# Layer 0's row maxima over 1024 keys at a time, ahead of each tile's scores, with value sums, totals and turns in the score banks

## The chip, the cores and the metric

One core of one Trainium2 chip runs the whole kernel. The metric is the device time of one execution in microseconds (us). The kernel is written in Bass and Tile: Tile places the tiles, records which instruction must wait for which, and sets semaphores; in layer 0's attention the order on TensorE (PE), VectorE (DVE) and ScalarE (ACT) is the order of the code, while GpSimd (POOL) and the DMA queue of SyncE (SP) are ordered by Tile's scheduler.

## The reference

Two attention layers over 1024 latent tokens and 256 context tokens of width 1024. Layer 0 is grouped-query attention with 16 heads of 64 and 4 key heads; a context token sees context keys only.

```python
def gqa_attend(q, k, v):
    s = jnp.einsum('bqhgd,bkhd->bhgqk', q, k).astype(jnp.float32) * (GQA_HEAD_DIM ** -0.5)
    p = jax.nn.softmax(s, axis=-1).astype(v.dtype)
    return jnp.einsum('bhgqk,bkhd->bqhgd', p, v)
...
    k_all = jnp.concatenate([kc, k], axis=1)
    v_all = jnp.concatenate([vc, v], axis=1)
    o = sweep_query_blocks(lambda qb: gqa_attend(qb, k_all, v_all), q).reshape(B, S, GQA_WIDTH)
    y = (o * jax.nn.silu(g)) @ p["w_out"]
...
        oc = gqa_attend(qc, kc, vc).reshape(B, L, GQA_WIDTH)
```

Around it stand RMS norms, projections, a SiLU gate and the output projection. Layer 1 is latent attention with 16 heads. Inputs and outputs are 32-bit floats.

## The kernel before

The attention of a layer is a list of units. Layer 0 has 20: 16 latent units, one for each head (10 key tiles of 128 keys against 1024 queries), and 4 context units, one for each key head (2 key tiles, 256 queries of 4 heads). They run as four latent units, one context unit, four, one, eight, and two context units at the end.

**A key tile.** `scores_by_halves` forms the scores, transposed: 128 keys by 1024 queries in a tile `st` of two PSUM banks, from a pool of two such tiles (`ps_s`). Each operand is split into a high and a low part of 64 rows, and the two halves of the queries lie on the two row halves of PE. So a tile has four products for each half (`QH,KA`, `QH,KB`, `QL,KA`, and `shift,minus`, which subtracts the row maximum), and a product of one half runs beside one of the other. ACT then writes the exponentials `p` out of `st` (line 508), which frees that buffer.

**The maxima.** The row maximum of a query over its keys is needed before the unit starts. The steps for units to come are cut into pieces and set between the products of the current unit (`next_maxima`, `max_parts`): one step is a product of 128 queries with 512 keys into a one-bank tile `mx` (`ps_m`, three of them), and a reduce over 512 on DVE. A latent unit has 16 such steps and 4 for the context keys, a context unit 4. Each key tile takes two steps, one for each row half: the one ahead of the first product of its half, the other behind the second product of the other half.

**The turn.** When a unit's maxima are done, `do_shift` reduces them to one value for each query; at the end of the unit that runs then, `turn` transposes them with PE into an `mx` tile (line 422), DVE casts them into the row `crow` (line 424, one buffer), and two small DMAs write the row into the unit's `shift` tile (line 427). There are four such tiles, used in turn.

**The end of a unit.** In this order: the turns; `pair_sum` on DVE, which adds the last four `p` by twos (line 528, four reduces); the totals of the unit before (line 597: PE sums the added `p` over the partitions into an `mx` tile, DVE transposes the result, line 601, and takes the reciprocal `cr`, line 602); then the value sums of this unit (`do_av`, line 555: 40 rows of the profile into the one-bank tile `av` of `ps_o`, one buffer), and `finish`, where ACT copies `av` to `os`. POOL adds the first six `p` and the pair sums meanwhile (`acp`, line 542), and scales the results.

Layer 0's PSUM is 3 banks of `ps_m`, 4 of `ps_s` and 1 of `ps_o`. While the gates before the attention are computed, `at.maxima` takes 36 steps ahead, and the unit loop starts with `at.run(28, 3, ...)`.

Of the kernel before, what the change touches and what calls it, by code (L numbers as in the profile page):

```python
# [26 lines left out]
TT = NT // P  # L27
EPS = 1e-6
HALVES = (True, True)


def raw(ap):
# [4 lines left out]
def hybrid_kernel(ctx: ExitStack, tc: tile.TileContext, ins: dict, out: bass.AP):  # L37
# [271 lines left out]
    class Attention:  # L309
        def __init__(self, l, units, ops):  # L310
            self.l, self.units, self.ops = l, units, ops
            self.state = {}
            self.vcache = {}
            self.kcache = {}
            self.sm = sm_pool
            self.step = 0
            self.deferred = []
            self.totals = []
            self.turns = []
            self.started = 0  # L320
            self.done = 0
            self.todo = []
            self.last_lat = [u for u in units if u["kind"] == "lat"][-1]
# [53 lines left out]
        def max_parts(self, u, step):  # L377
# [30 lines left out]
                return half, [part_ctx] + [lambda: None] * (self.ops["mparts"] - 1)  # L408
            return half, [lambda j=j: part(j) for j in range(self.ops["mparts"])]

        def do_shift(self, u):

            s = self.state[id(u)]
            if u["kind"] == "lat":
                m = self.sm.tile([P, 8], F32, name="m1", tag="m1")
                dve.reduce_max(m, s["m"], axis=AX.X)
            else:
                m = s["m"][:, :, 0]

            def turn():  # L420
                t = self.ps_m.tile([P, 512], F32, name="mx", tag="mx")[:8, :P]
                pe.transpose(t, m, ident)
                r = self.sm.tile([8, P], F32R, name="crow", tag="crow", bufs=1)
                dve.tensor_copy(r, t)
                if HALVES[self.l]:
                    for n in range(2):
                        sp.dma_start(raw(s["crow"][n]), raw(r[4 * n:4 * n + 4, :]))
                else:
                    sp.dma_start(raw(s["crow"]), raw(r))

            self.turns.append(turn)

        def start_unit(self):
            u = self.units[self.started]
            s = self.ops["load"](u, self)
            lat = u["kind"] == "lat"
            s["m"] = self.sm.tile([P, 8, 3 if lat else 1], F32, name="m", tag="m" if lat else "mc")
# [3 lines left out]
            if HALVES[self.l]:  # L441
                if lat:
                    self.todo += [(u, ("lat", i + 4 * a, n)) for i in range(4) for n in range(2) for a in range(2)]
                self.todo += [(u, ("ctx", i + 2 * a, 0)) for i in range(2) for a in range(2)]
            else:
                if lat:
                    self.todo += [(u, ("lat", i, n)) for i in range(8) for n in range(2)]
                self.todo += [(u, ("ctx", i, 0)) for i in range(4)]
            self.started += 1

        def next_maxima(self, upto, limit):

            steps = []
            while self.done < upto:
                if not self.todo and self.started < min(limit, len(self.units)):
                    self.start_unit()
                if not self.todo:
                    break
                u, m = self.todo.pop(0)
                self.done += 1  # L460
                half, parts = self.max_parts(u, m)
# [30 lines left out]
        def scores_by_halves(self, u, kt, p, steps):  # L492
# [15 lines left out]
            act.activation(p, ps, AF.Exp, scale=self.ops["scale"])  # L508
# [37 lines left out]
        def do_av(self, u, group, ps):  # L546
# [1 line left out]
            s = self.state[id(u)]  # L548
            kts = u["kts"]
            if group[0] == kts[0]:  # L550
                s["av"] = self.ps_o.tile([P, 512], F32, name="av", tag="av")
                s["v"] = self.load_v(u)
            for kt, p in zip(group, ps):
                for n in range(2):
# [16 lines left out]
        def finish(self, u):  # L571
# [19 lines left out]
            cr = sm.tile([P, 8], F32, name="cr", tag="cr")  # L591

            def total():
                t = s["av"] if u is not self.units[-1] and not HALVES[l] else self.ps_m.tile([P, 512], F32, name="mx", tag="mx")
                for i, part in enumerate(s["total"]):
                    for q in range(4):
                        pe.matmul(t[32 * q:32 * q + 32, :256], lhsT=twos, rhs=part[:, q * 256:q * 256 + 256],  # L597
# [31 lines left out]
        def run(self, lead, ahead, extra, tail):  # L629
# [3 lines left out]
            with tc.manual_schedule(engines={mybir.EngineType.PE, mybir.EngineType.DVE, mybir.EngineType.Activation}):  # L633
                for t, u in enumerate(self.units):
# [13 lines left out]
                    for group in (kts[:cut], kts[cut:]):  # L648
# [560 lines left out]

    def l0_open(at, st):  # L1210
        pool_ = st.enter_context(tc.tile_pool(name="shift0", bufs=1, **right))
        at.minus = pool_.tile([P, P], F32R, name="minus")
        at.shift = [pool_.tile([P, 512], F32R, name=f"shift{i}") for i in range(4)]
        for t in (at.minus, *at.shift):
            pool.memset(raw(t), 0.0)
        for n in range(2):
            pool.memset(raw(at.minus[64 * n:64 * n + 1, :]), -1.0)

    def l0_load_halves(u, at, lat, KH, KL):
        g = u["g"]  # L1220
        i = at.started % 4
        qp = at.qp if i < 3 else at.qp2
        QH = qp.tile([P, 512], F32R, name="QH", tag="QA")
        QL = qp.tile([P, 512], F32R, name="QL", tag="QB")
        for t, src in ((QH, q0h), (QL, q0l)):
            for n in range(2):
                dst = raw(t[64 * n:64 * n + 64, :])
                if lat:
                    h = u["h"]
                    sp.dma_start(dst, src[h // 2, 64 * (h % 2):64 * (h % 2) + 64, 512 * n:512 * n + 512])  # L1230
                else:
                    sp.dma_start(dst.rearrange("p (a n) -> p a n", a=2),
                                 src[2 * g:2 * g + 2, 64 * n:64 * n + 64, NL:].rearrange("a p n -> p a n"))
        X = at.shift[i]
        return dict(KH=KH, KL=KL, QH=QH, QL=QL, X=X, minus=at.minus, crow=[X[64 * n:64 * n + 1, :] for n in range(2)])

    def l0_load(u, at):
        kp = at.kp
# [38 lines left out]

    def l0_maxima(s, n):
        r = slice(64 * n, 64 * n + 64)
        return [(s["QH"][r, :], s["KH"][r, :])]  # L1280

    def l0_scores(s, kt, n=None):
        ks = slice(kt * P, (kt + 1) * P)
        if n is not None:
            r = slice(64 * n, 64 * n + 64)
            return [(s["KH"][r, ks], s["QH"][r, :]), (s["KL"][r, ks], s["QH"][r, :]),
                    (s["KH"][r, ks], s["QL"][r, :]), (s["minus"][r, :], s["X"][r, :])]
        return [(s["KA"][:, ks], lambda n: s["QA"][:, n * 512:(n + 1) * 512]),
                (s["KB"][:, ks], lambda n: s["QB"][:, n * 512:(n + 1) * 512])]
# [511 lines left out]
```

## Time and profile before

| | |
|---|---|
| three timed runs | 1706.63, 1708.12, 1713.32 us (median 1708.12) |
| the profiled execution, its own time | 1703.22 us |
| its span | 1701.4 us |
| mean granted TensorE clock | 0.997 |
| layer 0's attention | about 380 to 750 us of the span |

A row of the timeline has the start, the time from the first start to the last end of the equal instructions that follow each other, the engine, the line, the operation, output and inputs, partitions and elements, their count, and in brackets the idle time of the engine ahead of it and what ended that. Matmuls overlap in their pipeline, so two rows that start 0.23 us apart can each show 0.39. A row of a table by windows has the stretch, its length, the busy time of PE, PE's weight loads, DVE, ACT and POOL with the number of instructions, then the granted clock, the DMA engines' share and GB/s. A row of the waits has who waited for whom, the sum, the number of times and the longest.

### The profile page before, as it was taken

What the parts mean: (1) busy time and instruction counts of PE and PEld (TensorE: products, weight loads), DVE (VectorE), ACT (ScalarE), POOL (GpSimd) and SP (SyncE); (2) the same over time, 40 slices, a digit from 0 to 9 for tenths busy, and PEclk for the clock granted to TensorE, in tenths of its full rate; (3) what the DMA queues carried; (4) which work ended last, traced back from release to release, by engine and by line L of the source; (5) the groups of instructions that cost most, each with busy time, mean ns of one, the idle gap of its engine ahead of it and who ended that gap; (6) DMA issues with size and microseconds to landing.
All of it is one profiled execution on the core that took longest, in us unless ns stands there. A gap on an engine that the chain in (4) does not pass through costs nothing. (4 is left out here: it accounts for less than half of the span.)

```text
span 1701.4 us, 27386 instructions
## 1 busy us (share of the span) xinstructions
PE 1663.7 (98%) x10212; PEld 1195.3 (70%) x10212; DVE 1042.7 (61%) x1807; ACT 641.6 (38%) x943; POOL 961.3 (57%) x646
## 2 busy tenths in 40 slices
PE   8999999999999999999989999999999999999998
PEld 5776768775555555557878889886766667667587
DVE  3765552357788777725575657754778777777231
ACT  4642222124455544432244543330434434344310
POOL 2773441218789988753235555350668787787521
PEclk9999999999999999999999999999999999999999
DMA  9557854521242422146433766776565555653451
GB/s 312 171 149 241 257 171 149 152 81 45 63 120 63 112 63 61 36 132 214 135 98 111 230 198 183 215 206 150 130 144 134 132 122 118 145 126 90 121 166 73
DMA packets 219821, 238.97 MB, mean 140 GB/s; under 512 B 23016, under 2 KB 159192, under 8 KB 219688
## 3 DMA queue, kind: packets, MB, share of 16 engines
q1 hardware_dynamic: 219264, 237.11, 49.5%
q8 instruction: 81, 1.33, 0.3%
q14 instruction: 52, 0.43, 0.1%
q10 hardware_dynamic: 424, 0.11, 0.0%
HBM read 163.37 MB, written 73.63 MB: 139 GB/s over the span
## 5 line engine op out<-in xcount | busy, mean ns | idle before, releaser
L395 DVE TENSOR_REDUCE m<-mx 128x1 f32<-128x512 f32 x512 | 336.0, 687 | 176.6 <-PE mx L393 171.6
L508 ACT ACTIVATE p<-st 128x1024 f32<-128x1024 f32 x328 | 335.9, 1027 | 170.9 <-PE st L501 137.5
L542 POOL TENSOR_TENSOR acp<-acp,p 128x1024 f32<-128x1024 f32 x128 | 305.4, 2386 | 7.8
L555 PE MATMUL av<-p,v 128*64 128x512 f32 x1312 | 289.9, 595 | 0.0
L555 PEld LDWEIGHTS av<-p,v 128*64 128x64 f32 x1312 | 90.9, 137 | 180.5 <-issue 177.9
L542 POOL TENSOR_TENSOR acp<-p 128x1024 f32<-128x1024 f32 x34 | 81.4, 2397 | 149.0 <-ACT p L508 148.9
L542 POOL TENSOR_TENSOR acp<-acp,acd 128x1024 f32<-128x1024 f32 x60 | 141.9, 2365 | 22.3 <-DVE acd L528 19.2
L528 DVE TENSOR_REDUCE acd<-p 128x512 f32<-128x1024 f32 x124 | 144.6, 1219 | 7.8 <-ACT p L508 7.8
L136 POOL TENSOR_TENSOR wb<-wraw,wa 128x512 fp32r<-128x512 f32 (+3 forms) x73 | 96.1, 1335 | 78.7 <-ACT wa L157 78.6
L93 PE MATMUL mm<-wa,hh 128*128 128x512 f32 (+2 forms) x336 | 127.2, 379 | 1.7 <-ACT hh L890 1.7
L501 PE MATMUL st<-QH,KH 64*128 64x512 f32 x320 | 122.9, 407 | 1.0 <-DVE gth L303 1.0
L95 PE MATMUL mm<-wa,hl 128*128 128x512 f32 (+2 forms) x336 | 121.3, 361 | 1.4 <-DVE hl L893 1.4
L94 PE MATMUL mm<-wb,hh 128*128 128x512 f32 (+2 forms) x336 | 120.9, 360 | 0.0
L501 PE MATMUL st<-QH,KL 64*128 64x512 f32 x320 | 119.6, 395 | 0.0
L501 PE MATMUL st<-QL,KH 64*128 64x512 f32 x320 | 118.9, 392 | 0.0
L576 ACT COPY os<-av 128x512 f32<-128x512 f32 x36 | 21.1, 587 | 255.9 <-PE av L555 214.5
L93 PE MATMUL y<-wa,oh 128*128 128x512 f32 (+1 forms) x296 | 114.3, 386 | 1.0 <-DVE yt L750 1.0
L95 PE MATMUL y<-wa,ol 128*128 128x512 f32 (+1 forms) x296 | 113.7, 384 | 0.0
L94 PE MATMUL y<-wb,oh 128*128 128x512 f32 (+1 forms) x296 | 113.7, 384 | 0.0
L404 DVE TENSOR_REDUCE m<-mx 128x2 f32<-128x512 f32 x144 | 95.4, 688 | 24.1 <-PE mx L403 19.0
L393 PE MATMUL mx<-KH,QH 64*128 64x512 f32 x256 | 102.6, 407 | 0.3 <-DVE m L404 0.3
L93 PE MATMUL mm<-hh,wa 128*128 128x512 f32 x256 | 102.1, 399 | 0.4 <-DVE qt L1675 0.4
(240 smaller groups left out, 4016.0 us busy)
## 6 DMA issues: line engine op xcount, KB each, us to landing
mraw<-in_l_w_mod SPq DMA_DIRECT2D x64, 256.0 KB
wraw<-in_l_w_in SPq DMA_DIRECT2D x28, 512.0 KB
KH<-k1h SPq DMA_DIRECT2D x32, 320.0 KB
KL<-k1l SPq DMA_DIRECT2D x32, 320.0 KB
rb<-rrow SPq DMA_DIRECT2D x72, 128.0 KB
mraw<-in_l_w_mod SPq DMA_DIRECT2D x16, 512.0 KB
sgd<-gth SPq DMA_DIRECT2D x32, 256.0 KB
wraw<-in_l_w_out SPq DMA_DIRECT2D x16, 512.0 KB
```

What stands on the lines that cost most here:

```text
L93: pe.matmul(ps, lhsT=lh(k), rhs=rh(k), start=first and i == 0, stop=False)
L94: pe.matmul(ps, lhsT=lh(k), rhs=rl(k), start=False, stop=False)
L95: pe.matmul(ps, lhsT=ll(k), rhs=rh(k), start=False, stop=last and i == len(ks) - 1)
L136: eng.tensor_sub(lo, a, b)
L393: pe.matmul(held["m"][:, cs], lhsT=q[:, t * P:(t + 1) * P], rhs=k[:, ks], start=j == 0, stop=j == len(pairs) - 1)
L395: dve.reduce_max(s["m"][:, i, n:n + 1], held["m"], axis=AX.X)
L404: dve.reduce_max(s["m"][:, 2 * i:2 * i + 2, 2 if u["kind"] == "lat" else 0], m.rearrange("p (a b) -> p a b", a=2), axis=AX.X)
L501: pe.matmul(ps[:, n * 512:(n + 1) * 512], lhsT=lh, rhs=rh, start=j == 0, stop=j == last)
L508: act.activation(p, ps, AF.Exp, scale=self.ops["scale"])
L528: dve.reduce_sum(t[:, ns], p2.rearrange("p a n -> p n a")[:, ns, :], axis=AX.X)
L542: pool.tensor_add(t, a, b)
L555: pe.matmul(s["av"][64 * n:64 * n + 64, :], lhsT=s["v"][:, kt, u["vc"]:u["vc"] + 64], rhs=p[:, n * 512:(n + 1) * 512], start=kt == kts[0], ...
```

## The change

`WIDE` is set for layer 0 alone. A maximum step there is `wide_max`: both row halves form 128 queries against 512 keys each, side by side, into one `mx` tile of two banks, and one reduce goes over all 1024 keys (or, for the context keys, over four times 256). So Q lies whole on both row halves (`QA`, 1024 queries). A tile takes one wide step, and both its products stand ahead of the tile's scores (`at_` is 0). `ps_m` is two tiles of two banks and `ps_s` two of two; `ps_o` is gone. The value sums take a tile of the score pool (`av_tile`): the first bank is `av`, the second, `spare`, takes the turns and the totals. Once no maxima are left, the tile comes from `ps_m`. The four `shift` tiles become one with a row for each of four units, and `minus` becomes four selectors.

```diff
@@ open_early
-            self.ps_m = st.enter_context(tc.tile_pool(name=f"psm{l}", bufs=3 if HALVES[l] else 2, space=PSUM, side="right", reuse_waits="tile"))
+            self.ps_m = st.enter_context(tc.tile_pool(name=f"psm{l}", bufs=2 if WIDE[l] or not HALVES[l] else 3, space=PSUM, side="right", reuse_waits="tile"))
@@ open_late
-            for name in (("ps_s", "ps_o"), ("ps_o", "ps_s"))[l]:
+            for name in (("ps_s",) if WIDE[l] else ("ps_s", "ps_o"), ("ps_o", "ps_s"))[l]:
@@ new
+        def wide_max(self, u, step):
+            s = self.state[id(u)]
+            kind, i = step
+            held = {}
+
+            def part(n):
+                if n == 0:
+                    held["m"] = self.ps_m.tile([P, 1024], F32, name="mx", tag="mx")
+                m, (q, k) = held["m"], self.ops["maxima"](s, n)[0]
+                if kind == "lat":
+                    pe.matmul(m[:, n * 512:n * 512 + 512], lhsT=q[:, i * P:(i + 1) * P], rhs=k[:, n * 512:n * 512 + 512],
+                              start=True, stop=True)
...
+                if n == 0:
+                    return
+                if kind == "lat":
+                    dve.reduce_max(s["m"][:, i, 0:1], m, axis=AX.X)
...
+            return [[lambda n=n: part(n)] for n in range(2)]
+
+        def av_tile(self, u):
+            pool_, tag = (self.ps_s, "st") if self.todo or self.started < len(self.units) else (self.ps_m, "mx")
+            t = pool_.tile([P, 1024], F32, name="avt", tag=tag)
+            self.state[id(u)]["av"] = t[:, :512]
+            self.spare = t[:, 512:]
@@ turn
-                t = self.ps_m.tile([P, 512], F32, name="mx", tag="mx")[:8, :P]
+                if not WIDE[self.l]:
+                    t = self.ps_m.tile([P, 512], F32, name="mx", tag="mx")[:8, :P]
+                elif self.spare is None:
+                    t = self.ps_m.tile([P, 1024], F32, name="mx", tag="mx")[:8, :P]
+                else:
+                    t = self.spare[:8, 256:256 + P]
@@ scores_by_halves
-                at_ = (last + 2) // 2 if half else 0
+                at_ = (last + 2) // 2 if half and not WIDE[self.l] else 0
@@ total
-                t = s["av"] if u is not self.units[-1] and not HALVES[l] else self.ps_m.tile([P, 512], F32, name="mx", tag="mx")
+                if WIDE[l]:
+                    t = self.spare
...
@@ run
-                                count += 2
+                                count += 1 if WIDE[self.l] else 2
...
+                        if WIDE[self.l] and group[0] == kts[0]:
+                            self.av_tile(u)
                         self.run_turns()
@@ l0_open
-        at.shift = [pool_.tile([P, 512], F32R, name=f"shift{i}") for i in range(4)]
+        at.minus = pool_.tile([P, 4, P], F32R, name="minus")
+        at.shift = pool_.tile([P, 512], F32R, name="shift")
@@ l0_load_halves
-        QH = qp.tile([P, 512], F32R, name="QH", tag="QA")
+        QA = qp.tile([P, NL], F32R, name="QA", tag="QA")
...
+                sp.dma_start(dst, q0h[h // 2, r, :NL])
@@ before and at the unit loop
-                    at.maxima(at.done + 4, 2)
+                    at.maxima(min(at.done + 2, 14), 2)
-    at.run(28, 3, pieces, lambda: first.extend(fetch_first(0, 2)))
+    at.run(14, 3, pieces, lambda: first.extend(fetch_first(0, 2)))
```

What this makes of the order. In these rows a name carries the number of its buffer, and brackets tell on whose count an instruction waits. First PE in the last key tile but one of the second unit; before:

```order
L393 MATMUL mx_3869<-KA_2959,QH_3517 128x512 [waits DVE_49]
L501 MATMUL st_3868<-QH_3293,KA_2959 128x512 [waits Activation_49]
L501 MATMUL st_3868<-QH_3293,KA_2959 128x512
L501 MATMUL st_3868<-QH_3293,KB_2960 128x512 x2
L393 MATMUL mx_3876<-KA_2959,QH_3517 128x512 [waits DVE_49]
L501 MATMUL st_3868<-QL_3294,KA_2959 128x512 x2
L501 MATMUL st_3868<-shift1_2949,minus_2947 128x512 x2
```

And now the same tile:

```order
L424 MATMUL mx_3798<-KA_2954,QA_3457 128x512 [waits DVE_49]
L424 MATMUL mx_3798<-KA_2954,QA_3457 128x512
L551 MATMUL st_3797<-QA_3268,KA_2954 128x512 [waits Activation_49]
L551 MATMUL st_3797<-QA_3268,KA_2954 128x512
L551 MATMUL st_3797<-QA_3268,KB_2955 128x512 x2
L551 MATMUL st_3797<-QL_3269,KA_2954 128x512 x2
L551 MATMUL st_3797<-shift_2948,minus_2947 128x512 x2
```

The second maximum product moved out from between the scores to the front, ahead of the wait for the score buffer. Next PE at the end of that unit, where turn, totals of the unit before and value sums follow each other; before:

```order
L422 MATMUL mx_3900<-ident_70,m1_3829 8x128 [waits DVE_49]
L597 MATMUL mx_3914<-acp_3549,twos_77 32x256 [waits DVE_49,Pool_49]
L597 MATMUL mx_3914<-acp_3549,twos_77 32x256 x3
L555 MATMUL av_3924<-p_3723,v_3508 64x512 x4
L555 MATMUL av_3924<-p_3724,v_3508 64x512 x4
```

And now:

```order
L465 MATMUL avt_3825<-ident_70,m1_3757 8x128 [waits Activation_49]
L651 MATMUL avt_3825<-acp_3497,twos_77 32x256 [waits DVE_49,Pool_49]
L651 MATMUL avt_3825<-acp_3497,twos_77 32x256 x3
L606 MATMUL avt_3825<-p_3668,v_3448 64x512 [waits DVE_49]
L606 MATMUL avt_3825<-p_3668,v_3448 64x512 x3
L606 MATMUL avt_3825<-p_3669,v_3448 64x512 x4
```

All three write one tile, `avt_3825`; the turn waits for ACT, and the first value product has a wait on DVE that it did not have. Its value in the built program is DVE's count after `RECIPROCAL cr_3658`. DVE at the same place; before:

```order
L424 CAST crow_3902<-mx_3900 8x128 [waits DMAHW1_49,DMAHW0_49,PE_49]
L528 TENSOR_REDUCE acd_3906<-p_3726 128x512 [waits Activation_49,Pool_49]
L528 TENSOR_REDUCE acd_3906<-p_3726 128x512
L528 TENSOR_REDUCE acd_3909<-p_3727 128x512 [waits Activation_49,Pool_49]
L528 TENSOR_REDUCE acd_3909<-p_3727 128x512
L601 STREAM_TRANSPOSE mx_3914<-mx_3914 128x256 [waits DVE_49,PE_49]
L602 RECIPROCAL cr_3715<-mx_3914 128x8 [waits DVE_49]
```

And now:

```order
L467 CAST crow_3827<-avt_3825 8x128 [waits DMAHW7_49,DMAHW0_49,PE_49]
L578 TENSOR_REDUCE acd_3831<-p_3671 128x512 [waits Activation_49,Pool_49]
L578 TENSOR_REDUCE acd_3831<-p_3671 128x512
L578 TENSOR_REDUCE acd_3834<-p_3672 128x512 [waits Activation_49,Pool_49]
L578 TENSOR_REDUCE acd_3834<-p_3672 128x512
L655 STREAM_TRANSPOSE avt_3825<-avt_3825 128x256 [waits DVE_49,PE_49]
L656 RECIPROCAL cr_3658<-avt_3825 128x8 [waits DVE_49]
```

The order on DVE is the same; the tile that transpose and reciprocal work on is now the one of the value sums.

More of the change, by code (lines that the diff above doesn't have):

```diff
@@ L440, in start_unit @@
                 s.pop("rest")()
-            if HALVES[self.l]:
+            if WIDE[self.l]:
+                if lat:
+                    self.todo += [(u, ("lat", i)) for i in range(8)]
+                self.todo += [(u, ("ctx", i)) for i in range(2)]
+            elif HALVES[self.l]:
                 if lat:
@@ L460, in next_maxima @@
                 self.done += 1
+                if WIDE[self.l]:
+                    steps += enumerate(self.wide_max(u, m))
+                    continue
                 half, parts = self.max_parts(u, m)
@@ L550, in do_av @@
             if group[0] == kts[0]:
-                s["av"] = self.ps_o.tile([P, 512], F32, name="av", tag="av")
+                if not WIDE[self.l]:
+                    s["av"] = self.ps_o.tile([P, 512], F32, name="av", tag="av")
                 s["v"] = self.load_v(u)
@@ L593, in total @@
             def total():
-                t = s["av"] if u is not self.units[-1] and not HALVES[l] else self.ps_m.tile([P, 512], F32, name="mx", tag="mx")
+                if WIDE[l]:
+                    t = self.spare
+                else:
+                    t = s["av"] if u is not self.units[-1] and not HALVES[l] else self.ps_m.tile([P, 512], F32, name="mx", tag="mx")
                 for i, part in enumerate(s["total"]):
@@ L1211, in l0_open @@
         pool_ = st.enter_context(tc.tile_pool(name="shift0", bufs=1, **right))
-        at.minus = pool_.tile([P, P], F32R, name="minus")
-        at.shift = [pool_.tile([P, 512], F32R, name=f"shift{i}") for i in range(4)]
[L1214 to L1217, printed above, removed]
+        at.minus = pool_.tile([P, 4, P], F32R, name="minus")
+        at.shift = pool_.tile([P, 512], F32R, name="shift")
+        pool.memset(raw(at.shift), 0.0)
+        for i in range(4):
+            a, b = (ident[:, j:j + 1].broadcast_to([P, P]) for j in (i, 64 + i))
+            dve.scalar_tensor_tensor(at.minus[:, i, :], a, -1.0, b, op0=ALU.mult, op1=ALU.subtract)
     def l0_load_halves(u, at, lat, KH, KL):
@@ L1222, in l0_load_halves @@
         qp = at.qp if i < 3 else at.qp2
-        QH = qp.tile([P, 512], F32R, name="QH", tag="QA")
+        QA = qp.tile([P, NL], F32R, name="QA", tag="QA")
         QL = qp.tile([P, 512], F32R, name="QL", tag="QB")
[L1225 to L1235, printed above, removed]
+        for n in range(2):
+            dst = raw(QA[64 * n:64 * n + 64, :])
+            low = raw(QL[64 * n:64 * n + 64, :])
+            if lat:
+                h = u["h"]
+                r = slice(64 * (h % 2), 64 * (h % 2) + 64)
+                sp.dma_start(dst, q0h[h // 2, r, :NL])
+                sp.dma_start(low, q0l[h // 2, r, 512 * n:512 * n + 512])
+            else:
+                for par in range(2):
+                    sp.dma_start(dst[:, 512 * par:512 * par + 512].rearrange("p (a n) -> p a n", a=2),
+                                 q0h[2 * g:2 * g + 2, 64 * par:64 * par + 64, NL:].rearrange("a p n -> p a n"))
+                sp.dma_start(low.rearrange("p (a n) -> p a n", a=2),
+                             q0l[2 * g:2 * g + 2, 64 * n:64 * n + 64, NL:].rearrange("a p n -> p a n"))
+        X = at.shift
+        return dict(KH=KH, KL=KL, QA=QA, QL=QL, X=X, minus=at.minus[:, i, :],
+                    crow=[X[64 * n + i:64 * n + i + 1, :] for n in range(2)])
     def l0_load(u, at):
@@ L1279, in l0_maxima @@
         r = slice(64 * n, 64 * n + 64)
-        return [(s["QH"][r, :], s["KH"][r, :])]
+        return [(s["QA"][r, :], s["KH"][r, :])]
     def l0_scores(s, kt, n=None):
@@ L1285, in l0_scores @@
             r = slice(64 * n, 64 * n + 64)
-            return [(s["KH"][r, ks], s["QH"][r, :]), (s["KL"][r, ks], s["QH"][r, :]),
+            qh = s["QA"][r, 512 * n:512 * n + 512]
+            return [(s["KH"][r, ks], qh), (s["KL"][r, ks], qh),
                     (s["KH"][r, ks], s["QL"][r, :]), (s["minus"][r, :], s["X"][r, :])]
```

13 lines of the change are left out of this document (12 added, 1 removed).

## The prediction

> **What bounds the kernel now.** I read the page's totals first, then the busy time over layer 0's attention, then the timeline of one head on TensorE, ScalarE and VectorE, then the waits of that stretch.
>
> ```profile
> span 1701.4 us, 27386 instructions
> PE 1663.7 (98%) x10212; PEld 1195.3 (70%) x10212; DVE 1042.7 (61%) x1807; ACT 641.6 (38%) x943; POOL 961.3 (57%) x646
> ...
> 380.00:715.00 335.00, 333.46 (x2290) 186.61 (x2289) 261.74 (x415) 165.45 (x172) 292.46 (x141) 1.00 0.26 71
> ```
>
> PE never seems to rest: 333.46 of 335.00 us in the stretch from 380 to 715, which holds nearly all of layer 0's attention (second column PE; then PEld, DVE, ACT, POOL). POOL is at 292.46 and DVE at 261.74. But ends of matmuls are modelled, so a short stall hides in a "busy" row; it is seen in the starts. Here is one head (unit 13 of 20), from the end of the value sums before it to its own:
>
> ```profile
> 628.60 0.50 PE L393 MATMUL mx<-KA,QH 64*128 64x512 f32 x1
> ...
> 628.94 0.63 PE L501 MATMUL st<-QH,KB 64*128 64x512 f32 x2
> ...
> 639.05 0.50 PE L501 MATMUL st<-QH,KA 64*128 64x512 f32 x2
> 639.38 0.39 PE L501 MATMUL st<-QH,KB 64*128 64x512 f32 x2
> ...
> 640.31 0.39 PE L501 MATMUL st<-QH,KA 64*128 64x512 f32 x2
> 640.54 0.39 PE L501 MATMUL st<-QH,KB 64*128 64x512 f32 x2
> ...
> 641.55 0.27 PE L422 MATMUL mx<-ident,m 128*8 128x128 f32 x1
> 641.76 0.64 PE L597 MATMUL mx<-acp,twos 128*32 128x256 f32 x8
> 642.33 8.80 PE L555 MATMUL av<-p,v 128*64 128x512 f32 x40
> ```
>
> Two 64-row products on the two row halves start together, and a pair follows a pair after 0.23 us (640.31 to 640.54). A key tile has five pairs, 1.16 us of PE. The tile at 639.05 was held: its second pair comes 0.33 later instead of 0.23. ScalarE shows the pace:
>
> ```profile
> 630.17 2.10 ACT L508 ACTIVATE p<-st 128x1024 f32<-128x1024 f32 x2 [0.87 <-PE st L501]
> 632.77 2.13 ACT L508 ACTIVATE p<-st 128x1024 f32<-128x1024 f32 x2 [0.51 <-PE st L501]
> 635.38 2.13 ACT L508 ACTIVATE p<-st 128x1024 f32<-128x1024 f32 x2 [0.48 <-PE st L501]
> 637.97 2.13 ACT L508 ACTIVATE p<-st 128x1024 f32<-128x1024 f32 x2 [0.46 <-PE mx L393]
> ...
> PEld st L501 <- ACT p L508: 18.8, 59, 0.5
> ```
>
> Two tiles take 2.60 us (632.77, 635.38, 637.97), not 2 x 1.16 = 2.32. Every second tile waits for its score buffer: 59 waits on the exponential in the stretch. The loop is fill a buffer, exponentiate, refill, with two buffers; the second row maximum stands inside the fill and lengthens it. So PE sets the end, and 0.28 us per two tiles of it is this loop.
>
> DVE at the end of the same head:
>
> ```profile
> 641.86 0.28 DVE L424 CAST crow<-mx 8x128 fp32r<-8x128 f32 x1
> 642.07 4.65 DVE L528 TENSOR_REDUCE acd<-p 128x512 f32<-128x1024 f32 x4
> 646.65 0.44 DVE L601 STREAM_TRANSPOSE mx<-mx 128x256 f32<-128x256 f32 x1
> 647.12 0.21 DVE L602 RECIPROCAL cr<-mx 128x8 f32<-128x8 f32 x1
> 651.60 1.89 DVE L395 TENSOR_REDUCE m<-mx 128x1 f32<-128x512 f32 x3 [4.26 <-PE mx L393]
> ...
> DVE crow L424 <- DMA shift<-crow: 11.3, 4, 3.3
> ```
>
> The turn's cast, four pair sums, the total's transpose and its reciprocal run from 641.86 to 647.33, beside the value sums that started at 642.33. They cost nothing now, since no matmul waits for them.
>
> **The change: tiles.** The number of products is the same; both halves' maxima now form the first pair, so a fill is four pairs in a row. Before shows this fill at the layer's end, where no maxima are left:
>
> ```profile
> 718.95 0.50 PE L501 MATMUL st<-QH,KA 64*128 64x512 f32 x2
> ...
> 719.99 0.40 PE L501 MATMUL st<-QH,KA 64*128 64x512 f32 x2
> ...
> 721.36 0.50 PE L501 MATMUL st<-QH,KA 64*128 64x512 f32 x2 [0.29 <-ACT p L508]
> ...
> 723.73 0.50 PE L501 MATMUL st<-QH,KA 64*128 64x512 f32 x2 [0.25 <-ACT p L508]
> ```
>
> The held tiles start 2.41 and 2.37 us apart. The maximum pair fits into that hold (two tiles hold 2.32 of PE work), so I take 2.37 per two tiles; the ends are 2.32 and the present 2.60. In the clock of the head above: the first score pair stands at 628.94, the ninth tile at 628.94 + 4 x 2.37 = 638.42, and its buffer is free at 638.42 + 2.37 = 640.79.
>
> One reduce over 1024 keys replaces two of 512. No row shows it out of PSUM. Its bounds: a pair sum reads 1024 from SBUF in (646.65 - 642.07) / 4 = 1.15 us; and the three reduces at 651.60 follow each other after (1.89 - 0.69) / 2 = 0.60, with 0.69 for the last:
>
> ```profile
> L395 DVE TENSOR_REDUCE m<-mx 128x1 f32<-128x512 f32 x512 | 336.0, 687 | 176.6 <-PE mx L393 171.6
> ```
>
> That is 1.20 for two. Either is about a tile's 1.19, so I put it at nothing; it is the cover that is thin.
>
> **The change: the turn, the totals, the value sums.** This is the large term. All three now sit in one tile, which is taken from the score buffers after the last score. The built program puts three waits in: the turn waits for the exponential of the ninth tile; the totals wait for the turn's cast; and the first value product waits on DVE, at the count of the reciprocal of the totals in the same tile. DVE's order is unchanged, so the four pair sums stand between cast and reciprocal. Turn at 640.79, done 641.06, cast at 641.10 (0.04 later, as from 641.55 + 0.27 to 641.86). From cast to the reciprocal's end is 647.33 - 641.86 = 5.47, so the value sums start at 641.10 + 5.47 + 0.05 = 646.62 instead of 642.33: 4.29 later, with the 0.76 that the tiles gained already in it. PE idles from the totals' end (641.10 + 0.28 + 0.04 + 0.64 = 642.06) for 4.56 us. Everything behind it on PE moves along: the value sums and the next head. 14 of the 16 latent units have turn or pair sums and somebody's totals (not the first, which has no totals, and not the last, which has no turn): 14 x 4.29 = 60.1.
>
> In three of these 14, two or three turns follow each other, and each further cast waits for the DMA that empties the one-row buffer: the waits above, 11.3 us in four. They lay beside value sums, and now stand ahead of the reciprocal: +11.3. On SP's queue the row's DMAs stand behind one Q load instead of three; the Q loads that now follow them are needed a head later.
>
> **The change: the clock.** PE's new idle time is long enough to ask what the granted clock does:
>
> ```profile
> 879.51 2.82 PE L270 MATMUL tp<-ident,xt 128*128 128x128 f32 x12 [5.24 <-DVE xt L258]
> ...
> 877.39:880.80 3.41, 1.29 (x6) 1.29 (x7) 2.68 (x5) 2.29 (x4) 0.55 (x1) 0.50 0.74 229
> 880.80:884.20 3.40, 3.40 (x17) 3.40 (x16) 3.36 (x8) 2.40 (x7) 1.44 (x2) 0.50 0.52 146
> 884.20:887.60 3.40, 3.40 (x28) 3.40 (x27) 2.95 (x6) 1.17 (x5) 1.51 (x2) 1.00 0.60 170
> 1191.42:1194.83 3.41, 1.75 (x16) 1.23 (x14) 1.38 (x2) 0.00 (x0) 0.66 (x1) 1.00 0.78 225
> 1194.83:1198.24 3.41, 3.41 (x18) 3.04 (x17) 1.46 (x3) 1.57 (x2) 0.00 (x0) 0.50 1.13 299
> ```
>
> Behind a gap of 5.24 us the clock (third column from the right) is 0.50 for 6.8 us, of which PE worked 1.29 + 3.40 = 4.69 and lost half, 2.35. Behind 3.41 us in which PE was busy for 1.75 it is 0.50 for 3.41, a loss of 1.7. The new gap of 4.56 lies between, and I take the shorter step: 14 x 1.7 = 23.9. The ends are nothing and 14 x 2.35 = 32.9. The Trainium skill, "TensorE: Matmul & The Clock Gate", section Part 1, says that the clock halves after an idle window of about 3.4 us and returns after a busy one; the steps of 3.41 agree, the half-busy window does not.
>
> **The change: the rest.** The two context units in the middle and the last three value sums also wait for transpose and reciprocal, without pair sums between: the totals start, 0.64 + 0.04 + 0.47 + 0.21 + 0.05 = 1.41 later the value sums, instead of 0.57. 5 x 0.84 = 4.2, less a wait that goes:
>
> ```profile
> 463.75 0.64 PE L597 MATMUL mx<-acp,twos 128*32 128x256 f32 x8 [0.75 <-POOL acp L542]
> ```
>
> That is +3.5. The gate stage has 14 wide steps in place of 36 narrow ones, four pairs less: -0.9; they return in the first four tiles, which the buffers held anyway. The shift rows of all units lie in one tile, so a head's first shift product waits for the last row's DMA; it is issued at the cast and has the value sums' 8.80 us and the gap to land, where a cast now waits 3.3 at most. Q is loaded whole into both halves, 16 x 256 KB = 4 MB more, at a DMA share of 0.26: hidden. The four DVE operations that make the selectors lie in the gate stage. POOL's 292 us of work get a longer stage.
>
> Sum: 60.1 + 11.3 + 23.9 + 3.5 - 0.9 = +97.9, on the profiled execution's 1703.2: 1801. The three timed runs had a median 4.9 above that execution, so 1806 for a median; I say 1805.
>
> **The rivals.** *The value sums don't wait.* They lie in one bank and the totals in the next; if the wait for the reciprocal is met early, only the tiles' gain is left: 14 x 0.76 + 0.9 = -11.5, 1692, as a median 1697: faster. It is decided where the first value product starts: within 1 us of the totals or after the reciprocal. The Trainium skill, "PSUM — Partial Sum Buffer", section on bank collisions, asks for guards by bank and quadrant, which would allow this; no run here shows it. Against the rival: the wait stands in the program, and the four pair sums cannot be over before their 4.58 us. 3 in 100. If only the totals' wait for the casts binds, 641.10 + 0.28 + 0.04 + 0.57 = 641.99 against 642.33: 14 x -0.34 + 11.3 - 0.9 = +5.6, a median of about 1714, within 0.5%: 2 in 100.
>
> *The clock holds.* 97.9 - 23.9: 1777, as a median 1782. For it is this gap, behind which the clock stayed at 1.00 though PE was busy for 1.66 of 3.42 us:
>
> ```profile
> 980.76 0.63 PE L1506 MATMUL tp<-ident,kn 128*128 128x128 f32 x4 [1.89 <-DVE kn L1470]
> ...
> 979.79:983.21 3.42, 1.66 (x12) 1.46 (x13) 2.38 (x4) 2.87 (x4) 2.48 (x3) 1.00 0.91 278
> 983.21:986.62 3.41, 3.41 (x21) 3.41 (x20) 1.88 (x2) 0.69 (x1) 3.41 (x2) 1.00 0.85 222
> ```
>
> Against it: that gap is under half of the new one, and the one of 5.24 did halve it. 10 in 100.
>
> *Only a wholly idle step halves the clock.* A step of 3.41 fits whole into 4.56 us in (4.56 - 3.41) / 3.41 = a third of cases; 14 / 3 x 2 us = 9 in place of 24: 1786, as a median 1791. That is the rule of the Trainium skill, "TensorE: Matmul & The Clock Gate", section Part 1, taken at its word. Against it: the window with 1.75 busy. 12 in 100.
>
> *The tiles don't get faster,* since the wide reduce is dearer than two narrow ones or the maximum pair at the front waits for its buffer: 16 x 0.76 = 12 more, 1813, as a median 1818. For it: DVE at 1.15 to 1.20 per tile has no room. 13 in 100.
>
> **How the numbers follow.** 60 in 100 for the forecast. The range takes in the clock's two ends (-24, +9) and the tiles' (+12, and -0.05 x 4.5 x 16 = -4): 1778 to 1830; it leaves out the cases without the wait. A change of under 0.5% is about what a measurement can't tell from none: faster 0.03, same 0.02, slower 0.95.
>
> **What would show it.** Right: 14 first value products with some 4.5 us of idle PE ahead, ended by DVE's reciprocal; granted clock under 1 over all of layer 0's attention; exponentials 2.37 apart by twos; three units with 3 to 5 us more. Wrong: value sums within 1 us of the totals; tiles still at 2.60; a layer 1 that differs by more than a few us, which nothing here accounts for.

## The result, and the profile after

The changed kernel takes 1800.95 us (median of four runs, 1799.1 to 1803.95) against 1707.38 us before (1706.34 to 1713.32): a ratio of 1.0552, with an interval of 1.0532 to 1.0573. The forecast was 1805, slower. The profiled execution took 1800.35 us, 97.1 more than the one of before, where the sum of the prediction had +97.9.

From the page of the changed kernel, the totals and the row of the clock (one digit for each fortieth of the span, in tenths of full speed); below them the busy times over the stretch that was read before, 380 to 715 us, with the same columns:

```profile
span 1798.6 us, 27215 instructions
PE 1677.8 (93%) x10212; PEld 1195.1 (66%) x10212; DVE 1035.5 (58%) x1643; ACT 642.2 (36%) x943; POOL 958.5 (53%) x640
...
PEclk9999999998988898989999999999999999999999
...
380.00:715.00 335.00, 273.61 (x1767) 145.82 (x1765) 199.06 (x211) 128.85 (x135) 233.60 (x114) 0.90 0.27 71
```

PE has the same 10212 products, but in this stretch 1767 instead of 2290: it rests for 61 of 335 us, and its clock is at 0.90 instead of 1.00. The digits under 9 are all in layer 0's attention. Here is the unit that the prediction read (unit 13), on PE, then ACT, then DVE, from the timeline of the changed kernel:

```profile
705.58 0.27 PE L465 MATMUL avt<-ident,m 128*8 128x128 f32 x1
706.31 0.64 PE L651 MATMUL avt<-acp,twos 128*32 128x256 f32 x8 [0.46 <-DVE crow L467]
711.39 10.47 PE L606 MATMUL avt<-p,v 128*64 128x512 f32 x40 [4.44 <-DVE cr L656]
...
697.37 2.12 ACT L558 ACTIVATE p<-st 128x1024 f32<-128x1024 f32 x2 [0.30 <-PE st L551]
699.75 2.12 ACT L558 ACTIVATE p<-st 128x1024 f32<-128x1024 f32 x2 [0.25 <-PE st L551]
702.12 2.11 ACT L558 ACTIVATE p<-st 128x1024 f32<-128x1024 f32 x2 [0.25 <-PE st L551]
...
701.27 4.62 DVE L433 TENSOR_REDUCE m<-mx 128x1 f32<-128x1024 f32 x4
705.89 0.28 DVE L467 CAST crow<-avt 8x128 fp32r<-8x128 f32 x1
706.09 4.62 DVE L578 TENSOR_REDUCE acd<-p 128x512 f32<-128x1024 f32 x4
...
711.12 0.21 DVE L656 RECIPROCAL cr<-avt 128x8 f32<-128x8 f32 x1
```

The totals end in PE's row at 706.95. The four pair sums stand between the cast and the transpose, and the value sums start at 711.39, 0.06 us after the reciprocal's end at 711.33: PE idles 4.44 us. Two tiles take 2.38 us. Then the value sums take 10.47 us in place of 8.80. The waits of the whole stretch (380 to 820 us) name the same place, and nothing else that is large on PE:

```profile
PE avt L606 <- DVE cr L656: 63.2, 16, 4.5
...
PE avt L651 <- DVE crow L467: 13.2, 14, 2.8
DVE crow L467 <- DMA shift<-crow: 10.3, 4, 2.7
```

Why the value sums got longer stands in the windows of the changed kernel (third column from the right: granted clock):

```profile
707.95:711.36 3.41, 0.00 (x0) 0.00 (x0) 3.35 (x5) 0.00 (x0) 3.33 (x2) 1.00 0.62 155
711.36:714.77 3.41, 3.38 (x8) 1.00 (x10) 0.00 (x0) 0.00 (x0) 2.81 (x2) 0.50 0.16 44
...
677.23:680.64 3.41, 0.34 (x8) 0.00 (x0) 3.41 (x4) 0.00 (x0) 3.25 (x3) 1.00 0.44 118
680.64:684.05 3.41, 2.04 (x6) 0.77 (x8) 1.28 (x3) 0.00 (x0) 3.33 (x2) 0.50 0.36 97
684.05:687.46 3.41, 3.41 (x10) 0.95 (x8) 0.00 (x0) 0.00 (x0) 1.19 (x2) 0.50 0.29 77
687.46:690.87 3.41, 3.41 (x18) 1.08 (x16) 0.00 (x0) 0.00 (x0) 2.15 (x2) 1.00 0.16 45
...
550.94:554.35 3.41, 1.46 (x10) 0.55 (x8) 1.52 (x3) 2.93 (x4) 3.33 (x2) 1.00 0.25 77
```

A window in which PE is busy for 0.00 or 0.34 of 3.41 us is followed by one at 0.50, and so is the one with 1.46 (550.94; its value sums took 10.73). Behind a half-speed window with 3.38 us of work the clock is back (value sums of 10.47); behind one with 2.04 it is not, and a second follows (the unit at 682, 11.49). So the same gap costs one window or two by where it falls.

Where the 97 us are, from the starts and ends of the value sums in both traces ("tail" is the time from the end of one unit's value sums to the start of the next):

| term | before | after | measured | the sum had |
|---|---|---|---|---|
| start of the first value sums (gate stage, first tiles) | 383.98 | 378.04 | -5.9 | -0.9 |
| 11 tails with one turn, each | 13.63 to 13.66 | 17.87 to 17.93 | 11 x 4.25 = +46.8 | 11 x 4.29 = +47.2 |
| 3 tails with two or three turns | 13.99, 13.97, 14.22 | 20.85, 20.87, 23.24 | +22.8 | 3 x 4.29 + 11.3 = +24.2 |
| length of 14 value sums | 8.80 | 10.19 to 11.75, mean 10.92 | +29.7 | +23.9 |
| two context units in the middle | 3.83, 3.01 | 4.18, 4.18 | +1.5 | +3.5, with the next row |
| from there to the last value sums | 30.95 | 33.95 | +3.0 | |
| layer 1 and the rest | | | -0.6 | 0 |
| sum | | | +97.3 | +97.9 |

### The profile page after: what moved, and what is told of

Read it like the earlier page. It is cut to its first block, busy times and chain, and to the rows that moved or that the text cites. A ratio compares the mean times of both kernels' runs of the same rounds, so it can differ in the third digit from the quotient of the medians.

```text
span 1798.6 us, 27215 instructions
## 1 busy us (share of the span) xinstructions
PE 1677.8 (93%) x10212; PEld 1195.1 (66%) x10212; DVE 1035.5 (58%) x1643; ACT 642.2 (36%) x943; POOL 958.5 (53%) x640
## 5 line engine op out<-in xcount | busy, mean ns | idle before, releaser
L433 DVE TENSOR_REDUCE m<-mx 128x1 f32<-128x1024 f32 x128 | 150.7, 1221 | 172.2 <-PE mx L424 171.7
L606 PE MATMUL avt<-p,v 128*64 128x512 f32 x672 | 178.5, 692 | 66.5 <-DVE cr L656 64.9
L397 DVE TENSOR_REDUCE m<-mx 128x1 f32<-128x512 f32 x256 | 176.2, 691 | 96.9 <-PE mx L395 93.4
L606 PEld LDWEIGHTS avt<-p,v 128*64 128x64 f32 x672 | 53.1, 159 | 183.9 <-issue 108.1
L606 PE MATMUL av<-p,v 128*64 128x512 f32 x640 | 141.1, 595 | 0.0
L606 PEld LDWEIGHTS av<-p,v 128*64 128x64 f32 x640 | 44.4, 137 | 88.3 <-issue 87.7
```

The source lines that it names most:

```text
L397: dve.reduce_max(s["m"][:, i, n:n + 1], held["m"], axis=AX.X)
L433: dve.reduce_max(s["m"][:, i, 0:1], m, axis=AX.X)
L606: pe.matmul(s["av"][64 * n:64 * n + 64, :], lhsT=s["v"][:, kt, u["vc"]:u["vc"] + 64], rhs=p[:, n * 512:(n + 1) * 512], start=kt == kts[0], ...
```

## Experiments

Three of the six kernels are the changed kernel with one edit, two are the first of these with a second edit, and one is the kernel before with one edit. Kernels of one series were timed against the kernel before on the same chip: the first four (before: 1705.98 us), then the last two (1705.27).

**Tiles of their own.** Turns and totals go back into the two-bank `mx` tiles; the value sums stay in the score banks.

```diff
@@ av_tile
-            pool_, tag = (self.ps_s, "st") if self.todo or self.started < len(self.units) else (self.ps_m, "mx")
+            pool_, tag = (self.ps_s, "st") if self.todo or self.turns or self.started < len(self.units) else (self.ps_m, "mx")
@@ turn
-                elif self.spare is None:
-                    t = self.ps_m.tile([P, 1024], F32, name="mx", tag="mx")[:8, :P]
                 else:
-                    t = self.spare[:8, 256:256 + P]
+                    t = self.ps_m.tile([P, 1024], F32, name="mx", tag="mx")[:8, :P]
@@ total
-                    t = self.spare
+                    t = self.ps_m.tile([P, 1024], F32, name="mx", tag="mx")[:, :512]
```

> The change, with turns and totals back in tiles of the maxima's pool; the value sums stay in a tile of the score pool. Theory (the cost is that value sums wait for the reciprocal of totals in the same tile): no idle PE ahead of the value sums, clock 1.0 in layer 0, tail and tiles together 0.7 us shorter than before per latent unit, and the gate stage's 5.9 us stay: 14 x -0.7 - 5.9 = -16, a median of about 1691, ratio 0.990. Rival (value sums in the score buffers hold up the next unit's tiles or slow the value sums themselves): above 1707, with the second tile of a unit late.

Measured: 1694.08 us (1690.94 to 1698.14), a ratio of 0.993 (0.9913 to 0.9948). The whole loss is gone, 106.9 us against the changed kernel, and the kernel takes 0.7% less than before; the theory had about 1691. The end of a unit, PE's and DVE's rows from the timeline of this kernel:

```profile
651.42 0.27 PE L463 MATMUL mx<-ident,m 128*8 128x128 f32 x1
652.00 0.64 PE L649 MATMUL mx<-acp,twos 128*32 128x256 f32 x8 [0.30 <-DVE m L433]
652.57 8.80 PE L604 MATMUL avt<-p,v 128*64 128x512 f32 x40
...
651.97 4.68 DVE L576 TENSOR_REDUCE acd<-p 128x512 f32<-128x1024 f32 x4
...
657.05 0.21 DVE L654 RECIPROCAL cr<-mx 128x8 f32<-128x8 f32 x1
```

Pair sums, transpose and reciprocal are as long as they were and lie beside the value sums again, which start 0.57 after the totals and take 8.80. What made them wait was the shared tile alone. In seven of the 11 units with one turn (called plain from here on) the tails are 13.06 to 13.10, 0.56 less than before, though the turn comes 0.9 earlier: the totals now wait 0.30 us, until a reduce has emptied one of the two `mx` tiles. In the other four plain units the tails are 13.18 to 13.71, and the unit with three turns loses (16.50 instead of 14.22, and value sums of 9.69 behind a half-speed window). So from the first value sums to the end of the last, the attention takes 363.5 us against 366.0 before. Most of the 10.3 us between the spans (1691.1 and 1701.4) lie ahead of it: the first value sums start at 377.20, 6.8 earlier.

**The totals first.** In the changed kernel, totals, transpose and reciprocal are put ahead of the pair sums in the order; the tile stays shared.

```diff
@@ run
                         self.run_turns()
+                        while WIDE[self.l] and not final and self.totals:
+                            self.totals.pop(0)()
                         if late or final:
```

> The change, with the totals' code ahead of the pair sums, so that on DVE transpose and reciprocal stand right behind the turn's cast; the tile is still shared. Theory (four pair sums of 1.15 us stand inside the wait): the value sums start 0.5 us later than before instead of 4.25, 14 x 0.5 = 7, plus the casts' 11.3, the context units and the end 4.5, clock 3 x 1.7 = 5, less 5.9: +22, a median of about 1729. Rival (the wait is for the casts or for POOL, not for the pair sums): within 5 us of 1801.

Measured: 1726.03 us (1725.06 to 1728.11), a ratio of 1.012 (1.0104 to 1.0136). PE and then DVE at the end of a unit:

```profile
676.79 0.64 PE L651 MATMUL avt<-acp,twos 128*32 128x256 f32 x8 [0.46 <-DVE crow L467]
678.31 8.80 PE L606 MATMUL avt<-p,v 128*64 128x512 f32 x40 [0.88 <-DVE cr L656]
...
677.55 0.47 DVE L655 STREAM_TRANSPOSE avt<-avt 128x256 f32<-128x256 f32 x1 [0.90 <-PE avt L651]
678.05 0.21 DVE L656 RECIPROCAL cr<-avt 128x8 f32<-128x8 f32 x1
678.17 4.61 DVE L578 TENSOR_REDUCE acd<-p 128x512 f32<-128x1024 f32 x4
```

The wait for the reciprocal is still there, but it is 0.88 us and not 4.44, since the pair sums' 4.6 us stand behind it. In the 11 plain units the clock holds and the value sums take 8.80. So of the 107 us between the changed kernel and the one with own tiles, 75 are the pair sums inside the wait, with the lowered clock that they bring; 32 are the wait on the rest, and on the casts where several turns follow each other (tails of 17.39, 17.57 and 20.10).

**Work in the gap.** The changed kernel with 18 pairs of products that nobody reads, between totals and value sums of the 14 units. It does more work on PE, not less.

```diff
@@ run
+                        if WIDE[self.l] and whole and 0 < t < 17:
+                            x = self.ps_m.tile([P, 1024], F32, name="mx", tag="mx")
+                            for i in range(18):
+                                for n in range(2):
+                                    q, k = self.ops["maxima"](self.state[id(u)], n)[0]
+                                    pe.matmul(x[:, n * 512:n * 512 + 512], lhsT=q[:, :P], rhs=k[:, :512], start=True, stop=True)
                         self.do_av(u, group, ps)
```

> The change, with 18 pairs of 64-row products (4.2 us of PE work, their result is read by nobody) between totals and value sums of units 1 to 16. Theory (the value sums take 10 to 11.7 us because PE's idle time lowers its clock): the clock stays at 1.0 in the 11 units with one turn, their value sums take 8.8, 11 x 2.1 = 23 us less and more in the other three: a median of 1773 to 1780. Rival (they are slower because of work beside them, on DVE or in the same banks): 1801, or more if the filler is late.

Measured: 1781.18 us (1778.66 to 1784.56), a ratio of 1.0441 (1.0424 to 1.0457): 19.8 us less than the changed kernel, with 504 more products, and 1 us above the theory's range. A unit's end in this kernel, and the window of the gap:

```profile
667.01 0.64 PE L651 MATMUL avt<-acp,twos 128*32 128x256 f32 x8 [0.46 <-DVE crow L467]
667.58 4.39 PE L747 MATMUL mx<-KA,QA 64*128 64x512 f32 x36
672.20 8.80 PE L606 MATMUL avt<-p,v 128*64 128x512 f32 x40 [0.22 <-DVE cr L656]
...
668.62:672.03 3.41, 3.35 (x30) 2.44 (x26) 3.38 (x5) 0.00 (x0) 3.33 (x2) 1.00 0.01 4
```

The value sums still wait for the reciprocal, and the plain tails are 17.96 to 18.03. But all 14 value sums take 8.80. From the start of the first to the end of the last, the stretch is 446.8 us instead of 469.7: the 29.7 us are gone, and 5.8 come back in the three units with several turns (tails of 22.51, 23.77 and 24.47) and about 0.1 in each other one. (Its first value sums start 3.7 us later. That is no effect of the added products, which come later: in this execution the clock was 0.50 for 10.24 us near 25 us of the span, and it is 4.4 us behind at 43 us.) So the idle time of PE, and not the shared banks or another engine, makes the value sums long.

**The gate stage.** The kernel before, with three steps of maxima at a time in the gate stage instead of four.

```diff
-                    at.maxima(at.done + 4, 2)
+                    at.maxima(at.done + 3, 2)
```

> The kernel before, with three steps of the maxima instead of four behind each gate product group; the nine steps left out come in the first key tiles. Theory (the fourth step waits for a third buffer and lands alone among the gate products, where each change between 64-row and 128-row products costs 0.1 us): 9 x 0.86 = 7.7 less, back some 0.5 in the first tile: a median of about 1700, ratio 0.9955 to 0.997. Rival (the 5.9 us that the first unit's value sums came earlier are the missing pairs alone, or tiles): 0.9 us or nothing.

Measured: 1700.6 us (1697.07 to 1701.59), a ratio of 0.9965 (0.9953 to 0.9977); the first scores start 4.2 us earlier than before (367.31 against 371.52), and the first value sums 3.2 (380.79), as eight more maximum products now stand in the first unit. The executions are up to 1.7 us apart ahead of the stage already, so the stage is better read by itself: from one and the same gate product, shortly ahead of the first maximum (309.99 before, 311.32 here, 309.60 in the changed kernel), to the last one of the stage are 61.32 us before, 55.78 here and 55.52 in the changed kernel. So the nine steps left out shorten it by 5.5 us, 0.6 each and not the theory's 0.86. The reason is in two pieces of PE's timeline, first of the kernel before:

```profile
323.19 0.39 PE L95 MATMUL mm<-hh,wb 128*128 128x512 f32 x1
323.50 0.73 PE L393 MATMUL mx<-KA,QH 64*128 64x512 f32 x3
324.16 0.50 PE L93 MATMUL mm<-hh,wa 128*128 128x512 f32 x1
324.50 0.40 PE L94 MATMUL mm<-hl,wa 128*128 128x512 f32 x1
324.82 0.49 PE L393 MATMUL mx<-KA,QH 64*128 64x512 f32 x1
325.25 0.50 PE L95 MATMUL mm<-hh,wb 128*128 128x512 f32 x1
```

then of the changed kernel:

```profile
323.72 0.39 PE L96 MATMUL mm<-hh,wb 128*128 128x512 f32 x1
324.04 0.73 PE L424 MATMUL mx<-KA,QA 64*128 64x512 f32 x4
324.70 0.50 PE L94 MATMUL mm<-hh,wa 128*128 128x512 f32 x1
```

Three maximum products and four take the same time between two gate products: 324.16 - 323.19 = 0.97 and 324.70 - 323.72 = 0.98. The fourth step of before came alone, as it had to wait for one of three `mx` tiles, and took the stretch from 324.50 to 325.25: 0.75 instead of the 0.23 between gate products. The trace of before has nine such lone pieces in the gate stage, which take 4.35 us together beyond the 0.23 each; the gate product behind each is some 0.1 late too (324.16 to 324.50). Gate product to maximum product and back each shows 0.31 to 0.43 instead of 0.23. The Trainium skill, "TensorEngine Tiling (Array Packing)", section Key Properties, says that a change of the tiling mode drains the engine; the rows fit that, at 0.1 to 0.2 us a change, but no run here shows the draining itself.

**The second maximum between the scores again.** The version with own tiles, in which the second half's maximum returns to the middle of the tile; reduce and buffers stay wide.

```diff
-                at_ = (last + 2) // 2 if half and not WIDE[self.l] else 0
+                at_ = (last + 2) // 2 if half else 0
```

> The version with tiles of their own for turns and totals, with one edit: the maximum of the second half of the keys is taken again in the middle of the tile's scores, not in front of them; the reduction stays one of 1024 keys, and its buffers stay as in the changed kernel. Theory (the position alone shortened the fill): two tiles take about 2.60 us again instead of 2.38, 4 to 5 pairs a unit, so about +1.0 us in each of 14 to 16 units, about +14 to +16: 1708 to 1711, a ratio near 1.001 to 1.003. Rival (the shorter fill comes from the reduction over 1024 keys and its three buffers): no change against that version, about 1694, a ratio of 0.992 to 0.994.

Measured: 1713.0 us (1710.85 to 1715.18), a ratio of 1.0041 (1.0028 to 1.0054): 18.9 more than with own tiles alone, a little above the theory's 14 to 16, and far from the rival's nothing. ACT's pace, and PE's totals at the end of that unit:

```profile
658.05 2.13 ACT L556 ACTIVATE p<-st 128x1024 f32<-128x1024 f32 x2 [0.53 <-PE st L549]
660.66 2.13 ACT L556 ACTIVATE p<-st 128x1024 f32<-128x1024 f32 x2 [0.48 <-PE st L549]
663.25 2.14 ACT L556 ACTIVATE p<-st 128x1024 f32<-128x1024 f32 x2 [0.46 <-PE st L549]
...
667.87 0.64 PE L649 MATMUL mx<-acp,twos 128*32 128x256 f32 x8 [0.74 <-DVE m L433]
```

Two tiles take 2.60 again (658.05, 660.66, 663.25). A tail is 14.47 instead of 13.09: about 0.9 from the tiles, and 0.44 because the last reduce now ends later and the totals wait 0.74 for its tile instead of 0.30. It is also 0.8 longer than in the kernel before (13.64), where the totals did not wait. So it is the place of the product, ahead of the wait for the score buffer, that shortens the fill. One reduce over 1024 in place of two over 512, with its two wide tiles in place of three narrow ones, gains no time by itself.

**The totals ahead of the turns,** on top of own tiles:

```diff
+                        while WIDE[self.l] and not final and self.totals:
+                            self.totals.pop(0)()
                         self.run_turns()
```

> The version with tiles of their own for turns and totals, with one edit: the totals' products stand ahead of the turns of the row factors in TensorE's order, still behind the pair sums. Theory: the totals wait only for the pair sums, and run in the time in which the turns would wait for the casts on SP's queue; the reciprocal no longer ends behind the turns, so about 0.3 us less in front of the value sums in the units with one turn and about 3 us less in the one with three: about 1686 to 1690, a ratio of 0.988 to 0.991. Rival (the totals were bound by GpSimd's pair sums, and the turns fill that wait): the time stays at about 1694 or rises by 0.3 to 0.5 us a unit, 1694 to 1700.

Measured: 1696.91 us (1693.66 to 1697.86), a ratio of 0.9946 (0.9929 to 0.9962): not faster than own tiles alone, so the theory missed. The mechanism that it named is there: nine of the 11 plain tails are 12.69 to 12.75, 0.34 less, and the one with three turns is 13.84 instead of 16.50. Another wait took its place:

```profile
568.58 0.26 DVE L465 CAST crow<-mx 8x128 fp32r<-8x128 f32 x1
...
575.62 1.37 SPq L468 DMA_DIRECT2D shift<-crow  x2
...
577.55 0.40 PE L549 MATMUL st<-QL,KA 64*128 64x512 f32 x2
580.48 0.79 PE L549 MATMUL st<-shift,minus 64*128 64x512 f32 x2 [2.53 <-DMA shift<-crow]
...
582.68 1.03 PE L549 MATMUL st<-QA,KA 64*128 64x512 f32 x2
583.11 1.03 PE L549 MATMUL st<-QA,KB 64*128 64x512 f32 x2
```

The next unit's first shift product waits 2.53 us for a row of the shift tile that all units share, and PE then works at 0.43 us a pair instead of 0.23 (granted clock 0.50 from 581.78 to 585.19). That tail is 17.22 instead of 13.08, one other plain tail is 14.91, and the stretch from unit 16's value sums to the last ones is 33.93 instead of 30.99. From the first value sums to the last, the attention takes 365.6 us against 363.5 with own tiles. The prediction had costed that wait at nothing, with the value sums' 8.80 us and the gap as its cover. Here the row's DMAs are issued 6.8 us after the cast has ended (575.62, and 568.58 + 0.26), behind eight other transfers on SP's queue; with own tiles alone it is 2.8 at the same place (567.25 after 564.46). So it is mainly the order on that queue, and not the turn that comes about 1 us later in the unit, that uses up the cover; no run changed that order alone.

## Why the prediction was right

**The wait on the shared tile** was the main term, 4.29 us a unit, and it measured 4.25. It was read from the built order (a wait of the first value product on DVE's count after the reciprocal) and priced from rows of before. Own tiles remove it, and totals ahead of the pair sums shrink it to 0.88 us with the tile still shared. The rivals in which the value sums or all but the totals don't wait (1697 and 1714) fall with that. The value sums and the totals lay in different banks, so the wait is one that the program holds for the whole tile; guards by bank, of which the prediction quoted the Trainium skill ("PSUM — Partial Sum Buffer", section on bank collisions), would not have asked for it. No run tried the guards by bank on one shared tile.

**The casts' DMA waits** in three units: +24.2 with the wait, measured +22.8. Right.

**The tiles:** 2.37 forecast, 2.38 measured, and the reduce over 1024 from PSUM, which no row of before had shown, is inside its bounds: four take 4.62 us one behind the other (the row at 701.27), 1.16 each, against 1.15 and 1.20. That is under a tile's 1.19, and the pace of the tiles holds. The rival in which the tiles don't get faster (1818) falls; the second maximum back between the scores shows what it would have been.

**The clock** is one of two terms that were mis-sized. The prediction took one half-speed window a unit, 1.7 us of loss; the 14 units have 26 such windows, 5 with one, 6 with two and 3 with three, and the loss is 2.12 a unit, 29.7 in all, inside the ends that it gave (0 and 32.9). Two things were missing: a gap that spreads over two windows leaves the second too little busy to end the half speed (in this kernel's layer 0, up to 2.56 of 3.41 us did not do it, 2.82 did), and the three units with several turns idle for longer (their first casts wait, and they are the three with three windows). The rival in which the clock holds was wrong on its premise; the kernel with work in the gap shows the clock's share by itself. The rival by which only a wholly idle step halves the clock, the rule of the Trainium skill ("TensorE: Matmul & The Clock Gate", section Part 1), had a third of the 14 units; PE was wholly idle in the window ahead in 5 of 14, but all 14 were halved, behind windows with up to 1.66 us of work. The steps of 3.41 us, which the same section states, agree.

**The gate stage** is the other: -0.9 forecast, -5.9 measured, of which 0.4 lies ahead of the stage, where the two executions differ. The step that failed was to count four pairs less at 0.23 us. What counts there is how often maximum products break the gate products' row: 18 times before, seven times in the changed kernel. Without the nine lone pieces the kernel before has a stage 5.5 us shorter, and the changed kernel's is 5.8 shorter, so the lone pieces are nearly the whole. Two groups less, at 0.98 - 0.23 = 0.75 each, save about as much as the first group loses in the changed kernel: it waits 0.91 us for a load of `KA` and takes 2.39 us, where the first one of before takes 0.86. That part rests on the rows alone.

The two errors, +5.8 and -5.0, have opposite signs, so it is luck that the total is closer than these terms. The small rest was as forecast: the shift rows, the larger loads of Q and the selectors cost nothing that the trace of the changed kernel shows, though the shift rows have little to spare.

## What to carry to other kernels

Before buffers of several operations are joined into one tile, list who waits for whose count on that tile: the price is all the work that stands in order between the first user's result and the last one's, even if each touches a bank of its own. Ask of any new idle time on PE of some us how much work it leaves in a 3.41-us window, and add the slower windows behind it, here one to three. The limit is not sharp in these figures: 1.46 and 1.66 us of work were followed by half speed in the changed kernel, and 2.15 in the last kernel above (711.49), but 1.66 was not in the kernel before (979.79). The loss of this change (a shared tile) could be parted from its gains by a few lines: with tiles of their own for turns and totals the kernel takes 0.993 of the time before, 11.9 us less. Of these the kernel before gets 5.4 without the change, by three steps at a time in the gate stage; the attention itself, with the product moved ahead of the wait for a buffer, is 2.5 us shorter.

## What was not expected of the hardware

- PE at half speed lasted 3.41, 6.83 or 10.24 us behind the idle time at the ends of 14 units (4.0 to 4.5 us ahead of the value sums, and more ahead of the totals where several turns follow each other), and a window that was busy for 1.46 or 1.66 of 3.41 us was enough to start it.
- Three 64-row products between 128-row ones cost as much as four (0.97 and 0.98 us), and a single one 0.75 us, against 0.23 with none between.
